# Six edits to a one-core, two-block transformer kernel: a second filling projection, every second convolution's projection in the eighth PSUM bank, and four moves of loads, stores and transposes

## The chip, the cores and the metric

The kernel runs on one core of one Trainium2 chip. The metric is the device time of one execution in microseconds; it was taken in three runs. The engines are called PE (TensorE: matmuls and transposes; its weight loads are PEld), ACT (ScalarE), DVE (VectorE), POOL (GpSimd) and SP (SyncE, which here only issues DMAs).

## What is computed

Sequence 512, width 1024, fp32. The first block has two layers; the second block has one.

```python
def first_block(x, ...):
    for layer in range(2):
        h = fox_attention(x, ...) if layer == 0 else diff_attention(x, k1, k2, v, ...)
        x = layer_norm(DN_ALPHA * x + h, ...)
        f = conv_ffn(x, ffn_w_in[layer], ffn_conv_w[layer], ffn_conv_b[layer], ffn_w_out[layer])
        x = layer_norm(DN_ALPHA * x + f, ...)
        if layer == 0: k1, k2, v = shared_kv(x, kv_w, cos, sin)

def second_block(x, ...):
    h = rms_norm(x, norm1_pre)
    q, k, v, z, xbc, dt_raw, gates = split_cols(h @ w_in, IN_SPLITS)
    q, k = axial_rope(rms_norm(q, q_norm), ...), axial_rope(rms_norm(k, k_norm), ...)
    attn_out = gqa_attention(q, k, v) @ w_attn_proj          # 8 query heads, 2 key heads
    ssd_y = ssd_branch(z, xbc, dt_raw, ...)                  # 5-tap convolution, silu, SSD both ways
    ssd_out = ssd_y @ w_ssd_proj
    g_attn, g_ssd = split(sigmoid(gates), 2)
    x = x + rms_norm((g_attn * attn_out + g_ssd * ssd_out) @ w_out, norm1_post)
    gate, up = split(rms_norm(x, norm2_pre) @ w_gate_up, 2)
    return x + rms_norm((silu(gate) * up) @ w_down, norm2_post)
```

## The kernel before

The sequence is held as four tiles of 128 rows (`t` = 0 to 3). Each fp32 product is made of three matmuls, since each operand is split into a high and a low part: weights come by SP's queue into `raw` (3 buffers, 512 KB each), ACT rounds them to `whi` (L185) and DVE makes the rest `wlo` (L186), 4 buffers of each. Activations are split in the same way (`split`, L193 on ACT and L194 on DVE). The transposed activations `xTh`, `xTl` come from `to_T` (L330) or `to_T2` (L1510): eight PE transposes of a tile, then L193 and L194.

PSUM has eight banks in three pools: `mm` with 3 banks (`psum()`), `at` with 4 (`psa()`), and `ms` with the eighth (`psm()`).

A scheduler writes the order of each engine's instructions from the program's text; each engine then runs its own list in order, and semaphores hold an instruction until what it reads is there and what it writes is free. Two things in the text steer that order. `later(t, f)` puts off the transposes of tile t, and `need(t)` issues those that are due; in `xs` the call is `need(t - self.depth)`, with `depth` 2. And `weave` takes turns between generators, so that filling work goes between the steps of an attention head.

The places that the change touches, in the order of time:

- `ffn` (L829), in both layers of the first block: `hook()` (L853) issues the loads of constants that the next stage uses (`load1`, `load2`), on POOL's queue, at group g = 1 of the up-projection.
- `run`, the end of layer 1's feed-forward (`post`, around L1591): after the layer norm of tile t, x is stored to DRAM (`xd`) by POOL's queue, and POOL computes the `pow` of the next norm (L1381, called by `rstd2`).
- `gqa` (L909 on): one projection gives k, v (`kv_epi`) and the first four q heads (`qgroup`), each through `norm_rope`. Then `F0` = 1 step of the filling work `fill` is issued, then k's transposes (L950, copied to `KT` by ACT at L952), then the eight heads: q's transposes (L957), scores (L543 and L544), `max` (DVE L965), `exp` (ACT L966), reciprocal (DVE L968), scaling (ACT L971, DVE L973), transposes of the probabilities (L401, split by L193 and L194) and the product with v (L985 and L986). Between those steps `fill` gives three steps a head: `ssd_convs`, 12 calls of `ssd_conv` (a projection of 24 matmuls, L217 to L219, into a PSUM bank; then ACT L1021, DVE L1025 four times, ACT L1027, DVE L1028), and between them transposes and products in the `ms` bank (L1112, L1117, L1125, copied by L1127 or split). After them come two gate projections. `ssd_scalars` uses `ms` too (L1077, L1078, L1090).
- `block2`, its end: `w_out` in two halves of 512 columns; in the second, tile by tile, `epi` does two norms (ACT L1341, DVE L1342, L1347, ACT L1349, POOL's `pow` L1381, ACT L1353), puts the transposes off by `later`, and stores x by POOL's queue (L1356, two per tile). `ffn2` follows at once: its first projections (`ws_pairs`, first) need tiles 0 and 1 of `xTh`, then tiles 2 and 3.
- `ffn2`, its end: the last rows of `w_down`, tile by tile; in `last` each tile's x is read back (L1545, POOL's queue) into one of two buffers `x2`, then the final norm and sum (L1549, twice a tile) and the stores of the result (L1550, SP's queue).

Of the kernel before, what the change touches and what calls it, by code (L numbers as in the profile page):

```python
# [8 lines left out]
F32 = mybir.dt.float32  # L9
# [7 lines left out]
D = 1024  # L17
P = 128
# [62 lines left out]
class K:  # L81
# [747 lines left out]
    def ffn(self, l, pool, make_post, hook):  # L829
        nc, I = self.nc, self.I  # L830
        W1, W2 = I["ffn_w_in"][l], I["ffn_w_out"][l]

        def conv(ps, m):
            y = pool.tile([P, S], F32, tag="cy", name="cy", bufs=4 - l)
            nc.scalar.activation(y, ps, AF.Identity, scale=self.c1(f"cw{l}2", m), bias=self.c1(f"cb{l}", m))  # L835
            for j, o in ((1, 1), (0, 2)):
                nc.vector.scalar_tensor_tensor(out=y[:, o:], in0=ps[:, :S - o], scalar=self.c1(f"cw{l}{j}", m), in1=y[:, o:], op0=ALU.mult, op1=ALU.add)  # L837
            return y

        def w_in(g):  # L840
            gc = self.ws_load(W1, g * 256)
            vc = self.ws_load(W1, DFF + g * 256)
            R = pool.tile([P, 2048], F32, tag="R", name="R", bufs=1)
            for i, gp, vp in self.ws_pairs(gc, vc, g == 0):
                y = conv(gp, 2 * g + i)
                nc.scalar.activation(y, y, AF.Silu)
                v = conv(vp, KF + 2 * g + i)
                nc.vector.tensor_tensor(out=R[:, i * 512:(i + 1) * 512], in0=y, in1=v, op=ALU.mult)
            if g == 0:
                for t in range(NT):  # L850
                    nc.scalar.activation(self.x[:, t, :], self.x[:, t, :], AF.Copy, scale=ALPHA)
            if g == 1:
                hook()  # L853
            return R

        def last():
            post = make_post()
            self.sums = [self.sm.tile([P, 3], F32, tag="sums", name="sums") for _ in range(NT)]
            self.ns = 2
            return lambda c: self.res_epi(c * 512, 512, 1.0, c, post if c else None)  # L860

        self.st_out(pool, W2, self.x, False, w_in, last)


# [148 lines left out]
    def ssd_conv(self, m):  # L1013

        nc = self.nc
        W = self.I["w_in_2"][0]
        ch = self.ws_load(W, 1792 + m * P, P)
        ps = self.psum()
        self.ws_mm(ps, ch, 0, self.xh, self.xl)
        y = self.unit()  # L1020
        nc.scalar.activation(y, ps, AF.Identity, scale=self.c1("c2w2", m), bias=self.c1("c2b", m))  # L1021
        for j in (0, 1, 3, 4):
            o = j - 2
            a, b = max(0, -o), S - max(0, o)
            nc.vector.scalar_tensor_tensor(out=y[:, a:b], in0=ps[:, a + o:b + o], scalar=self.c1(f"c2w{j}", m), in1=y[:, a:b], op0=ALU.mult, op1=ALU.add)  # L1025
        th = self.unit()
        nc.scalar.activation(th, y, AF.Tanh)  # L1027
        nc.vector.scalar_tensor_tensor(out=y, in0=th, scalar=1.0, in1=y, op0=ALU.add, op1=ALU.mult)  # L1028
        return y
# [202 lines left out]
    def block2(self, bpool):  # L1232
        nc, I, tc = self.nc, self.I, self.tc
# [33 lines left out]
        with tc.tile_pool(name="L", bufs=self.NL) as self.L:  # L1267
# [31 lines left out]
            with tc.tile_pool(name="mix", bufs=1) as pool:  # L1299
# [39 lines left out]
                def epi(c, t, ps):  # L1339
# [3 lines left out]
                    if c == 1:  # L1343
                        r = self.rstd2(sst[t])
                        ss = self.sm.tile([P, 2], F32, tag="ss4", name="ss4")
                        for i in range(2):
                            nc.vector.scalar_tensor_tensor(out=x[t][i], in0=mo[t][i], scalar=r, in1=x[t][i], op0=ALU.mult, op1=ALU.add)  # L1347
                            jk = pool.tile([P, S], F32, tag="jk", name="jk")
                            nc.scalar.activation(jk, x[t][i], AF.Square, scale=1.0 / 32, accum_out=ss[:, i:i + 1])  # L1349
                            nc.vector.tensor_tensor(out=mo[t][i], in0=x[t][i], in1=G2[:, i * 512:(i + 1) * 512], op=ALU.mult)  # L1350
                        r = self.rstd2(ss)
                        for i in range(2):
                            nc.scalar.activation(mo[t][i], mo[t][i], AF.Copy, scale=r)  # L1353
                        self.later(t, lambda: self.to_T2(mo[t], t))
                        for i in range(2):
                            nc.gpsimd.dma_start(xd[t, i], x[t][i])  # L1356
                for c in range(2):
                    self.xs(I["w_out_2"][0], c * 512, 512, KD, lambda k: mx[k][0], lambda k: mx[k][1], lambda t, ps, c=c: epi(c, t, ps), stagger=4 if c else 0)
        with tc.tile_pool(name="ffn2", bufs=1) as pool:
            self.ffn2(pool)  # L1360

    NL = 38
    F0 = 1
    depth = 2

    @staticmethod
# [147 lines left out]
    def ffn2(self, pool):  # L1514
        nc, I = self.nc, self.I
# [18 lines left out]
        def last(c):  # L1534
            sl = slice(c * 512, (c + 1) * 512)

            def epi(t, ps):
# [3 lines left out]
                nc.scalar.activation(jk, a, AF.Square, scale=1.0 / 32, accum_out=sst[t][:, c:c + 1])  # L1541
                nc.vector.tensor_tensor(out=a, in0=a, in1=G[:, sl], op=ALU.mult)
                if c == 1:
                    xt[t] = pool.tile([P, D], F32, tag="x2", name="x2", bufs=2)
                    nc.gpsimd.dma_start(xt[t], xd[t])  # L1545
                    r = self.rstd2(sst[t])
                    for i in range(2):
                        s = slice(i * 512, (i + 1) * 512)
# [1 line left out]
                        nc.sync.dma_start(self.out[t * P:(t + 1) * P, s], xt[t][:, s])  # L1550
            return epi

        self.st_out(pool, W2, acc, True, w_in, lambda: last)

    def run(self):
        nc, I, tc = self.nc, self.I, self.tc
# [3 lines left out]
        with tc.tile_pool(name="xp", bufs=1) as xp:  # L1560
# [19 lines left out]
            with tc.tile_pool(name="ffn1", bufs=1) as pool:  # L1580
# [4 lines left out]
                def make():  # L1585
# [2 lines left out]

                    def post(t):
                        self.layer_norm(t, G, B, jk)  # L1590
                        nc.gpsimd.dma_start(xd[t], self.x[:, t, :])  # L1591
                        h = pool.tile([P, D], F32, tag="Q", name="Q", bufs=4)
                        ss = self.sm.tile([P, 2], F32, tag="ss4", name="ss4")
                        for i in range(2):
# [39 lines left out]
```

## Time and profile before

| | |
|---|---|
| median of 3 runs | 2091.38 us (2090.37 to 2091.85) |
| the profiled execution | 2091.34 us |
| its span in the trace | 2089.6 us |
| granted TensorE clock, mean over the span | 0.995 |
| PE busy | 2038.2 us (98%) |
| DVE, ACT, POOL busy | 74%, 52%, 4% |

The trace shows the span; the profiled execution is 1.7 us longer than that. A row of a timeline gives an instruction's start, its duration and, in brackets, how long its engine had been idle before it and whose end released it. A matmul's duration is that of a pipelined instruction: the next one starts before it ends, so the step from start to start is what one costs. In `<-` the output stands on the left.

### The profile page before, as it was taken

How to read it: one execution, taken by the hardware profiler on the slowest of the kernel's cores; microseconds unless marked ns; L12 is line 12 of the kernel's file. 1: busy time of each engine (PE TensorE's matmuls, PEld its weight loads, DVE VectorE, ACT ScalarE, POOL GpSimd, SP SyncE). 2: the span in 40 equal slices, each digit the busy share in tenths (PEclk: the TensorE clock that was granted, in tenths of full speed). 3: DMA queues.
4: the chain of work that ended last, by engine and by line, in shares of the span. 5: the costliest groups of instructions: out<-in, count | busy, mean ns of one | idle time of the engine just before them, and what ended most of it. 6: DMA issues, size and time to landing. Idle time of an engine off the chain costs nothing.

```text
span 2089.6 us, 28051 instructions
## 1 busy us (share of the span) xinstructions
PE 2038.2 (98%) x10563; PEld 1724.7 (83%) x10563; DVE 1554.7 (74%) x2776; ACT 1085.3 (52%) x1905; POOL 75.6 (4%) x113
## 2 busy tenths in 40 slices
PE   8999999999999999999999998999999999999998
PEld 7888888888888789888888887887898878888886
DVE  5777878788956888777887866997798544575564
ACT  4777655444435977455444344676475343443322
POOL 0000000000000000010000011000000010000000
PEclk9999999999999999999999999999999999999999
DMA  6221242233223221252224332211323425222322
GB/s 170 62 61 61 71 139 85 77 121 121 84 88 91 71 71 51 66 166 83 76 86 131 101 117 78 72 31 36 106 61 98 144 91 185 97 90 72 121 81 91
DMA packets 197470, 193.71 MB, mean 93 GB/s; under 512 B 8934, under 2 KB 170455, under 8 KB 197335
## 3 DMA queue, kind: packets, MB, share of 16 engines
q1 hardware_dynamic: 191398, 173.04, 26.9%
q0 software_dynamic: 5504, 17.31, 2.7%
q8 instruction: 83, 1.36, 0.3%
q10 hardware_dynamic: 432, 1.57, 0.2%
q14 instruction: 53, 0.43, 0.1%
HBM read 185.61 MB, written 6.29 MB: 92 GB/s over the span
## 4 chain that ended last, share of the span: by engine, by line
PE 80%; DVE 8%; ACT 7%; issue 3%; POOL 1%; DMA 1%; POOLq 0%; DVEq 0%; ACTq 0%; SPq 0%
PE mm L219 15%; PE mm L218 15%; PE mm L217 15%; PE mm L293 3%; PE mm L291 3%; PE mm L292 3%; PE at L1437 3%; PE at L1438 3%; PE at L1439 3%; PE at L401 2%; DVE wlo L186 1%; ACT sw L699 1%; PE mm L1437 1%; PE mm L1438 1%; PE mm L1439 1%
## 5 line engine op out<-in xcount | busy, mean ns | idle before, releaser
L217 PE MATMUL mm<-xTh,whi 128*128 128x512 f32 (+1 forms) x1584 | 605.4, 383 | 8.2 <-ACT xTh L193 5.6
L219 PE MATMUL mm<-xTh,wlo 128*128 128x512 f32 (+1 forms) x1584 | 604.2, 382 | 1.2 <-DVE wlo L186 1.2
L218 PE MATMUL mm<-xTl,whi 128*128 128x512 f32 (+1 forms) x1584 | 604.6, 382 | 0.1
L185 ACT ACTIVATE whi<-raw 128x1024 fp32r<-128x1024 f32 (+3 forms) x282 | 293.2, 1044 | 316.2 <-PE mm L218 174.6
L186 DVE TENSOR_TENSOR wlo<-raw,whi 128x1024 fp32r<-128x1024 f32 (+3 forms) x282 | 337.1, 1199 | 146.0 <-ACT whi L185 140.2
L217 PEld LDWEIGHTS mm<-xTh,whi 128*128 128x128 f32 x1584 | 298.9, 189 | 63.3 <-ACT xTh L193 6.1
L219 PEld LDWEIGHTS mm<-xTh,wlo 128*128 128x128 f32 x1584 | 298.8, 189 | 57.6 <-DVE wlo L186 2.1
L218 PEld LDWEIGHTS mm<-xTl,whi 128*128 128x128 f32 x1584 | 299.1, 189 | 54.7 <-DVE xTl L194 0.3
L837 DVE SCALAR_TENSOR_TENSOR cy<-mm,cols,cy 128x511 f32<-128x511 f32 (+1 forms) x172 | 128.3, 746 | 67.3 <-ACT cy L835 65.3
L193 ACT ACTIVATE whi<-wr 128x1024 fp32r<-128x1024 f32 x84 | 89.0, 1060 | 90.2 <-PE mm L218 29.1
L293 PE MATMUL mm<-whi,xTl 128*128 128x256 f32 x416 | 119.0, 286 | 1.7 <-DVE xTl L194 1.0
L291 PE MATMUL mm<-whi,xTh 128*128 128x256 f32 x416 | 119.2, 287 | 1.1 <-ACT xTh L193 1.1
L835 ACT ACTIVATE cy<-mm,cols 128x512 f32<-128x512 f32 x86 | 66.5, 773 | 103.1 <-PE mm L219 103.1
L292 PE MATMUL mm<-wlo,xTh 128*128 128x256 f32 x416 | 118.3, 285 | 0.0
L194 DVE TENSOR_TENSOR wlo<-wr,whi 128x1024 fp32r<-128x1024 f32 x84 | 101.9, 1220 | 12.9 <-ACT whi L193 12.0
L193 ACT ACTIVATE hh<-R 128x256 fp32r<-128x256 f32 (+2 forms) x57 | 54.9, 963 | 85.4 <-DVE R L1528 43.2
L1438 PE MATMUL at<-wlo,hh 128*128 128x512 f32 x240 | 93.4, 389 | 0.0
L1439 PE MATMUL at<-whi,hl 128*128 128x512 f32 x240 | 93.4, 389 | 0.0
L1437 PE MATMUL at<-whi,hh 128*128 128x512 f32 x240 | 92.7, 389 | 0.0
L193 ACT ACTIVATE ph<-at 128x512 fp32r<-128x512 f32 (+3 forms) x128 | 58.6, 474 | 54.2 <-PE at L401 40.7
L293 PEld LDWEIGHTS mm<-whi,xTl 128*128 128x128 f32 x416 | 80.2, 193 | 3.4 <-DVE xTl L194 1.9
L291 PEld LDWEIGHTS mm<-whi,xTh 128*128 128x128 f32 x416 | 80.2, 193 | 2.6 <-ACT xTh L193 1.8
(451 smaller groups left out, 3850.5 us busy)
## 6 DMA issues: line engine op xcount, KB each, us to landing
raw<-in_ffn_w_in_dram SPq DMA_DIRECT2D x88, 512.0 KB
raw<-in_w_gate_up_dram SPq DMA_DIRECT2D x44, 512.0 KB
raw<-in_w_in_dram SPq DMA_DIRECT2D x40, 512.0 KB
wr<-in_ffn_w_out_dram SPq DMA_DIRECT2D x32, 512.0 KB
raw<-in_a_w_in_dram SPq DMA_DIRECT2D x22, 512.0 KB
raw<-in_kv_w_dram SPq DMA_DIRECT2D x16, 512.0 KB
wr<-in_w_down_dram SPq DMA_DIRECT2D x16, 512.0 KB
raw<-in_ffn_w_out_dram SPq DMA_DIRECT2D x12, 512.0 KB
```

The source lines that it names most:

```text
L185: nc.scalar.activation(hi, raw, AF.Copy)
L186: nc.vector.tensor_tensor(out=lo, in0=raw, in1=hi.bitcast(F32), op=ALU.subtract)
L193: nc.scalar.activation(hi, src, AF.Copy)
L217: mm(o, wh, a, start=(k == 0), stop=False)
L218: mm(o, wh, b, start=False, stop=False)
L219: mm(o, wl, a, start=False, stop=(k == ktiles - 1))
L291: mm(o, a, hi[:, kk, :], start=(k == 0 and t % 2 == 0), stop=False)
L292: mm(o, a, lo[:, kk, :], start=False, stop=False)
L293: mm(o, b, hi[:, kk, :], start=False, stop=(k == ktiles - 1 and t % 2 == 1))
L1437: mm(ps[t], a, wh, start=p == 0, stop=False)
L1438: mm(ps[t], a, wl, start=False, stop=False)
L1439: mm(ps[t], b, wh, start=False, stop=p == 1)
```

## The change

- `hook()` is called at g = 4 instead of g = 1.
- `ssd_conv` takes its bank from `ms` for odd m, from `mm` for even m (the order of the calls is m = 8, 10, 0, 1, 2, 3, 9, 11, 4, 5, 6, 7).
- `F0` is 2: two filling projections are issued ahead of k's transposes.
- x is stored from SP's queue instead of POOL's, in layer 1's `post` and in `block2`'s `epi`.
- `depth` is 1 from `w_out` on.
- The four reads of x at the end of `ffn2` are issued together ahead of the last projection (`ends`), into two tiles of the ring `R`; the buffers `x2` are gone.

```diff
--- before.py
+++ after.py
@@ -849,7 +849,7 @@
             if g == 0:
                 for t in range(NT):
                     nc.scalar.activation(self.x[:, t, :], self.x[:, t, :], AF.Copy, scale=ALPHA)
-            if g == 1:
+            if g == 4:
                 hook()
             return R
 
@@ -1015,7 +1015,7 @@
         nc = self.nc
         W = self.I["w_in_2"][0]
         ch = self.ws_load(W, 1792 + m * P, P)
-        ps = self.psum()
+        ps = self.psm() if m % 2 else self.psum()
         self.ws_mm(ps, ch, 0, self.xh, self.xl)
         y = self.unit()
         nc.scalar.activation(y, ps, AF.Identity, scale=self.c1("c2w2", m), bias=self.c1("c2b", m))
@@ -1353,14 +1353,15 @@
                             nc.scalar.activation(mo[t][i], mo[t][i], AF.Copy, scale=r)
                         self.later(t, lambda: self.to_T2(mo[t], t))
                         for i in range(2):
-                            nc.gpsimd.dma_start(xd[t, i], x[t][i])
+                            nc.sync.dma_start(xd[t, i], x[t][i])
+                self.depth = 1
                 for c in range(2):
                     self.xs(I["w_out_2"][0], c * 512, 512, KD, lambda k: mx[k][0], lambda k: mx[k][1], lambda t, ps, c=c: epi(c, t, ps), stagger=4 if c else 0)
         with tc.tile_pool(name="ffn2", bufs=1) as pool:
             self.ffn2(pool)
 
     NL = 38
-    F0 = 1
+    F0 = 2
     depth = 2
 
     @staticmethod
@@ -1541,8 +1542,6 @@
                 nc.scalar.activation(jk, a, AF.Square, scale=1.0 / 32, accum_out=sst[t][:, c:c + 1])
                 nc.vector.tensor_tensor(out=a, in0=a, in1=G[:, sl], op=ALU.mult)
                 if c == 1:
-                    xt[t] = pool.tile([P, D], F32, tag="x2", name="x2", bufs=2)
-                    nc.gpsimd.dma_start(xt[t], xd[t])
                     r = self.rstd2(sst[t])
                     for i in range(2):
                         s = slice(i * 512, (i + 1) * 512)
@@ -1550,7 +1549,15 @@
                         nc.sync.dma_start(self.out[t * P:(t + 1) * P, s], xt[t][:, s])
             return epi
 
-        self.st_out(pool, W2, acc, True, w_in, lambda: last)
+        def ends():
+            for i in range(2):
+                R = pool.tile([P, 2048], F32, tag="R", name="R", bufs=2)
+                for t in (2 * i, 2 * i + 1):
+                    xt[t] = R[:, t % 2 * D:(t % 2 + 1) * D]
+                    nc.gpsimd.dma_start(xt[t], xd[t])
+            return last
+
+        self.st_out(pool, W2, acc, True, w_in, ends)
 
     def run(self):
         nc, I, tc = self.nc, self.I, self.tc
@@ -1588,7 +1595,7 @@
 
                     def post(t):
                         self.layer_norm(t, G, B, jk)
-                        nc.gpsimd.dma_start(xd[t], self.x[:, t, :])
+                        nc.sync.dma_start(xd[t], self.x[:, t, :])
                         h = pool.tile([P, D], F32, tag="Q", name="Q", bufs=4)
                         ss = self.sm.tile([P, 2], F32, tag="ss4", name="ss4")
                         for i in range(2):
```

PE in the middle of the eight heads, around the first products of `ssd_scalars` (L1077); L217 to L219 on `mm` are filling projections. Before:

```order
L217 MATMUL mm<-xTh,whi 128x512
L986 MATMUL at<-pl,L 128x512
L543 MATMUL at<-L,A 128x512
L544 MATMUL at<-L,A 128x512
L985 MATMUL at<-ph,L 128x512
L218 MATMUL mm<-xTl,whi 128x512
L1077 MATMUL ms<-L,c_sums 128x64 x2
L1078 MATMUL ms<-L,c_sums 128x128
L219 MATMUL mm<-xTh,wlo 128x512
L543 MATMUL at<-L,A 128x512
L544 MATMUL at<-L,A 128x512
L217 MATMUL mm<-xTh,whi 128x512
```

After (line numbers before L1356 are the same):

```order
L543 MATMUL at<-L,A 128x512
L986 MATMUL at<-pl,L 128x512
L544 MATMUL at<-L,A 128x512
L957 MATMUL at<-ident,L 128x128 x4
L401 MATMUL at<-ident,Pt 128x128 x8
L1077 MATMUL ms<-L,c_sums 128x64 x2
L1078 MATMUL ms<-L,c_sums 128x128
L985 MATMUL at<-ph,L 128x512
L986 MATMUL at<-pl,L 128x512
L543 MATMUL at<-L,A 128x512
L544 MATMUL at<-L,A 128x512
L985 MATMUL at<-ph,L 128x512
```

Before, matmuls of a filling projection stand between the steps of the head; after, at this place, none do from the L401 rows ahead of this piece on until the projection into `ms` that follows it. Over the whole program PE has as many instructions as before, and so have DVE and ACT.

ACT from the second half of `w_out` into `ffn2` (L1341, L1349, L1353: the epilogue of a tile; L193 `xTh`: the split of a transposed tile; L185: weights). Before:

```order
L1353 ACTIVATE L<-L,ss_16064 128x512 x2
L1341 ACTIVATE jk,ss_15859<-mm 128x512
L1349 ACTIVATE jk,ss_16103<-L 128x512 x2
L1353 ACTIVATE L<-L,ss_16113 128x512 x2
L1341 ACTIVATE jk,ss_15860<-mm 128x512
L193 ACTIVATE xTh<-at 128x4x128 x2
L185 ACTIVATE whi<-raw 128x1024
L1349 ACTIVATE jk,ss_16152<-L 128x512
L185 ACTIVATE whi<-raw 128x1024
L1349 ACTIVATE jk,ss_16152<-L 128x512
L185 ACTIVATE whi<-raw 128x1024
L1353 ACTIVATE L<-L,ss_16162 128x512 x2
```

After:

```order
L1353 ACTIVATE L<-L,ss_16064 128x512 x2
L1341 ACTIVATE jk,ss_15859<-mm 128x512
L193 ACTIVATE xTh<-at 128x4x128 x2
L1349 ACTIVATE jk,ss_16103<-L 128x512 x2
L1353 ACTIVATE L<-L,ss_16113 128x512 x2
L1341 ACTIVATE jk,ss_15860<-mm 128x512
L193 ACTIVATE xTh<-at 128x4x128 x2
L185 ACTIVATE whi<-raw 128x1024
L1349 ACTIVATE jk,ss_16166<-L 128x512
L185 ACTIVATE whi<-raw 128x1024
L1349 ACTIVATE jk,ss_16166<-L 128x512
L185 ACTIVATE whi<-raw 128x1024
```

Before, the first split of a transposed tile comes after the third tile's L1341 and the second (three rows further on) after the third tile's L1353; after, the splits of tiles 0 and 1 come behind the L1341 of tiles 1 and 2. On PE the eight transposes of tile 0 stand behind 48 matmuls of the second half instead of 72.

POOL at the end of `ffn2` (`ss` rows: one `pow` per tile). Before:

```order
L1381 TENSOR_TENSOR ss_16225<-ss_16224,mhalf 128x1
L353 DMA G<-in_norm_post_dram 128x1024
L1545 DMA x_18667<-xd 128x1024
L1545 DMA x_18700<-xd 128x1024
L1381 TENSOR_TENSOR ss_18670<-ss_18669,mhalf 128x1
L1381 TENSOR_TENSOR ss_18703<-ss_18702,mhalf 128x1
L1545 DMA x_18733<-xd 128x1024
L1381 TENSOR_TENSOR ss_18736<-ss_18735,mhalf 128x1
L1545 DMA x_18766<-xd 128x1024
L1381 TENSOR_TENSOR ss_18769<-ss_18768,mhalf 128x1
```

After, where L1381 is L1382 and L1545 is L1557:

```order
L1382 TENSOR_TENSOR ss_16239<-ss_16238,mhalf 128x1
L353 DMA G<-in_norm_post_dram 128x1024
L1557 DMA R<-xd 128x1024 x4
L1382 TENSOR_TENSOR ss_18674<-ss_18673,mhalf 128x1
L1382 TENSOR_TENSOR ss_18705<-ss_18704,mhalf 128x1
L1382 TENSOR_TENSOR ss_18736<-ss_18735,mhalf 128x1
L1382 TENSOR_TENSOR ss_18767<-ss_18766,mhalf 128x1
```

The four reads stand ahead of all the `pow`s. On SP's queue the eight stores L1356 stand among the loads of `ffn2`: three loads, six stores, three loads, two stores, two loads.

## Rows read from the trace of the kernel before

**Rows 1.** Page, part 1: busy time of each engine and share of the span.

```profile
PE 2038.2 (98%) x10563; PEld 1724.7 (83%) x10563; DVE 1554.7 (74%) x2776; ACT 1085.3 (52%) x1905; POOL 75.6 (4%) x113
```

**Rows 2.** PE timeline, w_out to ffn2: start us, us, instruction, idle before it.

```profile
1707.12 0.39 PE L257 MATMUL mm<-whi,L 128*128 128x512 f32 x1
...
1712.57 1.03 PE L1510 MATMUL at<-ident,L 128*128 128x128 f32 x8
...
1725.25 0.98 PE L217 MATMUL mm<-xTh,whi 128*128 128x256 f32 x3 [5.31 <-ACT xTh L193]
...
1740.62 0.62 PE L217 MATMUL mm<-xTh,whi 128*128 128x256 f32 x3 [0.30 <-ACT xTh L193]
```

**Rows 3.** Windows, all engines: length, busy us, then PEclk, DMA share, GB/s.

```profile
1236.00:1266.00 30.00, 26.54 (x191) 23.90 (x191) 24.68 (x47) 17.07 (x37) 7.13 (x11) 1.00 0.37 121
1271.00:1274.60 3.60, 3.60 (x19) 3.60 (x19) 1.69 (x4) 0.05 (x1) 1.65 (x1) 0.55 0.72 192
1299.00:1302.50 3.50, 3.50 (x14) 3.11 (x13) 0.00 (x0) 3.48 (x7) 0.00 (x0) 0.56 0.00 0
1360.00:1400.00 40.00, 40.00 (x214) 32.55 (x213) 38.17 (x74) 28.99 (x71) 0.00 (x0) 1.00 0.05 15
1725.00:1729.00 4.00, 3.75 (x18) 3.75 (x19) 3.87 (x8) 3.38 (x7) 1.67 (x3) 0.57 1.02 332
```

**Rows 4.** ACT timeline, the same stretch.

```profile
1707.60 1.34 ACT L1353 ACTIVATE L<-L,ss 128x512 f32<-128x512 f32 x2 [1.11 <-POOL ss L1381]
...
1714.45 1.34 ACT L1353 ACTIVATE L<-L,ss 128x512 f32<-128x512 f32 x2 [1.11 <-POOL ss L1381]
...
1722.80 1.33 ACT L1353 ACTIVATE L<-L,ss 128x512 f32<-128x512 f32 x2 [0.85 <-POOL ss L1381]
...
1724.61 1.07 ACT L193 ACTIVATE xTh<-at 128x512 fp32r<-128x512 f32 x2
```

**Rows 5.** POOL timeline, the stores at 1257 and 1705, and the last issue of the tail.

```profile
1257.86 0.58 POOL L1591 DMA_DIRECT2D xd<-x  x1 [1.74 <-DVE x L381]
1258.83 0.56 POOL L1381 TENSOR_TENSOR ss<-ss,mhalf 128x1 f32<-128x1 f32 x1 [0.39 <-DVE ss L1380]
...
1705.21 1.21 POOL L1356 DMA_DIRECT2D xd<-L  x2 [1.08 <-DVE L L1347]
1707.00 0.56 POOL L1381 TENSOR_TENSOR ss<-ss,mhalf 128x1 f32<-128x1 f32 x1 [0.58 <-DVE ss L1380]
...
2080.57 0.57 POOL L1545 DMA_DIRECT2D x<-xd  x1 [1.84 <-DMA out_dram<-x]
```

**Rows 6.** SP queue timeline, start of ffn2.

```profile
1722.41 8.67 SPq L183 DMA_DIRECT2D raw<-in_w_gate_up_dram  x4
```

**Rows 7.** DVE timeline, the tail.

```profile
2070.02 1.42 DVE L1549 SCALAR_TENSOR_TENSOR x<-acc,ss,x 128x512 f32<-128x512 f32 x2 [0.74 <-POOL ss L1381]
...
2082.24 0.15 DVE L1380 SCALAR_TENSOR_TENSOR ss<-ss 128x1 f32<-128x1 f32 x1
2084.76 1.42 DVE L1549 SCALAR_TENSOR_TENSOR x<-acc,ss,x 128x512 f32<-128x512 f32 x2 [2.37 <-issue]
```

**Rows 8.** PE timeline around k's transposes, 1269 to 1299.

```profile
1269.09 1.99 PE L950 MATMUL at<-ident,L 128*128 128x128 f32 x8 [2.35 <-ACT L L923]
...
1297.58 0.47 PE L217 MATMUL mm<-xTh,whi 128*128 128x512 f32 x1 [1.21 <-DVE L L1025]
1298.70 0.69 PE L957 MATMUL at<-ident,L 128*128 128x128 f32 x2 [0.64 <-ACT L L952]
```

**Rows 9.** DVE timeline, reciprocals of two successive heads.

```profile
1425.67 0.18 DVE L968 RECIPROCAL s<-s 128x4 f32<-128x4 f32 x1 [0.65 <-ACT Pt L966]
...
1436.79 0.18 DVE L968 RECIPROCAL s<-s 128x4 f32<-128x4 f32 x1 [0.59 <-ACT Pt L966]
```

**Rows 10.** ACT and DVE by line, 1304 to 1450: xcount, busy us, mean ns, idle before.

```profile
L1021 ACT ACTIVATE L<-mm,cols 128x512 f32<-128x512 f32 x10 | 7.8, 779 | 0.0
...
L1127 ACT ACTIVATE L<-ms 128x128 f32<-128x128 f32 x32 | 6.4, 293 | 1.3 <-PE ms L1125 1.2
...
L1025 DVE SCALAR_TENSOR_TENSOR L<-mm,cols,L 128x510 f32<-128x510 f32 (+1 forms) x44 | 32.6, 740 | 1.0 <-ACT L L1021 0.9
```

**Rows 11.** Waits of PE, 1225 to 1450: us, times, longest.

```profile
PE at L401 <- DVE Pt L973: 0.8, 1, 0.8
```

## Prediction

> **What bounds the kernel.** I read the page's first part, then PE's waits, then the timelines of the three places where the change moves PE's work or the end of the program. PE is busy 98% of the span [rows 1], so the reader should look for the little that PE does not do: a stall of PE, what arrives last at it, and what the clock does afterwards. No instruction is added on PE, DVE or ACT; only order, queues and banks move. The three places are **A**, the grouped attention of the second block (1225 to 1450 us), **B**, the passage from `w_out` into `ffn2` (1707 to 1741), and **C**, the tail.
>
> Two things hold for all of them. First, a 128x512 matmul costs 0.227 us: 24 of them run from 1707.12 to 1712.57 [rows 2]. Eight 128x128 transposes take 1.03 us as a row [rows 2], of which the last one's overlap is hidden; about 0.108 us each. Second, a long stall costs twice. After the idle 2.35 us before L950 [rows 8] the granted clock is 0.55 over the next 3.6 us, and after the 5.31 us of B [rows 2] it is 0.57 over 4 us, which is its lower level (1.2 of 2.4 GHz) for most of that time [rows 3]; about 3.4 us at half speed loses 1.7 us. The stretch 1236 to 1266 holds 3.5 us of idle PE in smaller pieces and keeps the clock at 1.00 [rows 3].
>
> **The change part by part, against the profiled execution of 2091.34 us** (the median of the runs shown is 2091.38, so the two agree to 0.04).
>
> *Hook.* The order of every engine is the same there with g = 4 as with g = 1: the loads wait for their memory, not for their place in the text. Cost and gain 0.
>
> *Stores from SP instead of POOL.* A pair of stores holds POOL for 1.21 us, a single one for 0.58 [rows 5]. The `pow` behind them would profit if it waited for them, but in both places POOL is idle 0.58 and 0.39 us before it and DVE's sum releases it [rows 5]. So the stores are already covered: 0. On SP they stand in front of weight loads; at `ffn2` the six stores follow three loads, and the fourth load starts at 1722.41 [rows 6], while tile 2's x is ready at about 1718.9: tile 0's pair starts at 1705.21 [rows 5], and a tile takes 6.85 us (L1353 at 1707.60 and 1714.45 [rows 4]). Six issues have 3.5 us to go out. Cost 0 as well. The bounds: nothing gained, nothing lost; if this cover were gone, one tile's chain would move by at most the 1.21 us pair.
>
> *B, depth 1.* Before, tile 1's transposes are ready by 1720, but their split L193 stands on ACT behind L1353 of tile 2, which runs 1722.80 to 1724.13; so L193 starts at 1724.61 [rows 4] and PE stands 5.31 us, then 0.30 us more at 1740.62 [rows 2]. With the lost clock B costs 5.31 + 0.30 + 1.7 = 7.3 us. After, the transposes of a tile come one tile earlier, and the splits stand ahead of the next tile's norms. PE is free after 48 matmuls at 1707.12, and tile 0's normed halves are there at 1708.27 and 1708.94 (L1353, two instructions from 1707.60 [rows 4]): with the first four transposes run in between, a wait of 1.45 us. The next 24 matmuls end at 1714.9; tile 1's L1353 ends at 1715.79: 0.5 us. The last 24 end at 1721.75, and the first products of `ffn2` follow, with some 0.3 us for a low part of the weights. Tile 2's transposes then meet a norm that ends at about 1724.8 (0.7 us later than now, since L1341 of tile 3 goes first): 1.4 us. Together 3.65 us, in pieces that are each shorter than the stalls after which rows 3 show a low clock. **B: -3.6 us**; -1.9 if a low stretch comes again, -4.5 if tile 2 is as early as now.
>
> *C, early reads.* The last read is issued at 2080.57 after a wait of 1.84 us for a store to free its buffer [rows 5], and the last L1549 starts at 2084.76, with 2.37 us idle before it [rows 7]. In the other tiles L1549 starts 0.9 us after L1380 (its 0.15 us and 0.74 of waiting for `pow` [rows 7]); L1380 of the last tile is at 2082.24, so with x there it starts at 2083.14. **C: -1.6 us.** The reads now go out ahead of the last projection, whose 144 matmuls of 0.227 us last 32.7 us, eight times the 4.2 us from the last issue to L1549. The bounds: 0 if the ring `R` were not free until then, 2.37 if `pow` were not needed.
>
> *A, filling projection and eighth bank.* Three terms.
>
> (1) The filling projections come earlier, and those in the shared bank wait for its other users, so that one head runs out of filling. From the last score of the head before it to its own last score, of which the piece of PE's order shows the end, PE has 26 matmuls of 128x512 (ten of them filling, all in front) and 20 transposes: 26 x 0.227 + 20 x 0.108 = 8.06 us. How fast a head can go when PE has little else is seen near the end of the heads: from reciprocal to reciprocal 1425.67 to 1436.79, 11.1 us [rows 9]. Cost 11.1 - 8.06, **+3.1 us**. At the very place, 0.43 us of transposes (L957 x4) stand between the last score and the L401 that wait for its softmax. Bounds: 0, if PE arrives so late that the softmax is ready; 4.8, if the stall also lowers the clock.
>
> (2) The `ms` bank is a single one, now with six projections in a row with its transposes. After such a projection it is held for L1021 and four L1025, 0.78 + 4 x 0.74 = 3.74 us [rows 10], before the next user may write; after L1125 for four copies L1127 of 0.29 [rows 10]. The order puts 3.8 to 6.8 us of PE work between a projection and the next user of the bank, so the bank is just about free in time; DVE's own queue, busy 38.17 of 40 us in the middle of the heads [rows 3], makes it late by some tenths. I take +0.3 us for each of the six, **+1.8**, with 0 and 6 (1 us each) as ends.
>
> (3) What may be gained. The wait for k's norms, 2.35 us, stays: L950 comes at the same place as before, and its releaser L923 depends on the projection, not on filling [rows 8]. The wait of 1.21 us for L1025 at 1297.58 [rows 8] is for one of the three `mm` banks; after, the fourth filling projection in `mm` waits for the same bank, so it stays, and the 0.64 us behind it too. One wait of 0.8 us for the scaled probabilities [rows 11] gets more work in front of it. **-0.8.**
>
> The Trainium skill, Perfetto Trace Analysis, Matmul Optimizations, says that all eight PSUM banks should be used, to have most work ready at a time; that would turn (1) and (2) into gains. No run here shows a projection in the eighth bank, and by that rule the time is that of the first rival.
>
> A: 3.1 + 1.8 - 0.8 = **+4.1 us**. Sum: 2091.34 - 3.6 - 1.6 + 4.1 = **2090.2 us**. Its own range, with A from +1 to +6 and B from -4.5 to -1.9: 2086.2 to 2093.8.
>
> **The rivals.** *The eighth bank pays* (faster). The stretch without filling costs nothing, since the stalls that I expect in the heads are hidden by PE's arriving later, and the bank is never late: 2091.34 - 3.6 - 1.6 - 0.8 = 2085.3. If the stall at 1297.58 goes as well, with its 1.21, 0.64 and the 1.7 of the low clock behind it (0.56 from 1299 [rows 3]), it is 2081.8. For it: that wait is truly for a bank. Against it: the piece of the order without filling.
>
> *The eighth bank starves PE* (slower). Each of the six projections in `ms` makes its next user wait 1 us, and the bare stretch ends in a low clock: 6 + 3.1 + 1.7 = 10.8, so 2091.34 - 5.2 + 10.8 = 2096.9. It decides from A = +9.4. For it: DVE is busy 95% of the time from 1360 to 1400 [rows 3], so 3.74 us are the least. Against it: the bank's occupation (six times 5.4 + 3.7, and the small users) is well below the 146 us of the heads.
>
> *B's waits merge.* If tiles 0 to 2 stall PE so that the clock falls again, B gives 1.9: 2091.34 - 1.9 - 1.6 + 4.1 = 2091.9, no change.
>
> *The change does nothing in B*: the order shows the moves, so only if tile 2's norm is late by 5 us; it is within the last rival.
>
> **How the numbers follow.** About 0.2% (4.2 us) is what a measurement of this kernel can tell from no change: faster is below 2087.2, slower above 2095.6. Chances: my forecast 0.48, the bank pays 0.26, the bank starves PE 0.15, B merges 0.11. Faster: nearly all of the first rival and the lowest eighth of the forecast, 0.31; slower: most of the second rival and a remainder, 0.15; the same 0.54. The range reaches into both rivals, from 2084.0 to 2096.0 and leaves out the outer parts of both, about 0.17.
>
> **What would show it.** The 5.31 us wait of L217 gone, with waits of 0.3 to 1.5 us at L1510 (then L1511) in its place and PEclk 1.00 behind them; the last L1549 (L1548 after the change) 0.9 us behind DVE's L1380 (then L1381); the waits for L950 and L1025 still there; and a new wait of about 3 us at L401 where the order has no filling. I am wrong if PE's waits inside the heads add up to nothing (first rival), or if PE waits for L1025 or L1127 at L1112, L1125 or at a projection into `ms` by more than 3 us in all (second).

## The result, and the profile after

The changed kernel takes 2122.7 us (median of 4 runs, 2121.58 to 2123.91) against 2091.43 for the kernel before on the same chip (4 runs): a ratio of 1.0151, interval 1.0139 to 1.0164. It is slower by 31.3 us, far above the range of the prediction. The profiled execution took 2121.63 us, its span 2119.6, with a mean granted clock of 0.992.

The page's part 1, after:

```profile
PE 2050.5 (97%) x10563; PEld 1731.1 (82%) x10563; DVE 1556.0 (73%) x2776; ACT 1086.1 (51%) x1905; POOL 68.6 (3%) x101
```

Against [rows 1] every engine has the work that it had, but for the twelve stores that SP's queue has taken over from POOL, and PE runs the same number of instructions. So the two traces can be laid side by side: the start of PE's n-th instruction after, less that of its n-th before, tells how late the changed kernel is there. (The order within a stretch differs, so this is read at the ends of the stretches.)

| PE's place, us of the trace after | late by, us | what PE has passed by then |
|---|---|---|
| 1200 | +0.3 | the hook; layer 1's `post` is next |
| 1277 | +0.4 | F0 = 2, k's transposes |
| 1322 | +2.2 | first head |
| 1372 | +14.9 | heads 2 to 4 |
| 1422 | +26.6 | heads 5 and 6 |
| 1475 to 1730 | +35.3 | end of the heads; then nothing until `w_out` |
| 1769 | +31.7 | **B** |
| 2074 | +31.6 | `ffn2` |
| end of span | +30.0 | **C** |

So A is +35, B is -3.6 and C -1.6. All of the loss lies in the heads. The next lines are windows of the trace after, cut where PE is at the same instruction as at 1320, 1357, 1395 and 1439.70 before (columns: length, busy us with instructions of PE, PEld, DVE, ACT, POOL, then PEclk, DMA share, GB/s):

```profile
1322.20:1371.90 49.70, 41.80 (x204) 31.14 (x202) 40.31 (x84) 28.65 (x64) 4.13 (x4) 0.93 0.20 53
1371.90:1421.60 49.70, 42.49 (x200) 33.31 (x199) 29.56 (x56) 23.51 (x51) 0.00 (x0) 0.97 0.11 28
1421.60:1475.00 53.40, 46.78 (x225) 35.15 (x222) 39.20 (x67) 32.64 (x76) 0.00 (x0) 0.97 0.13 34
```

and the same three of the kernel before:

```profile
1320.00:1357.00 37.00, 35.83 (x204) 29.65 (x204) 33.08 (x70) 23.39 (x51) 4.15 (x4) 1.00 0.27 72
1357.00:1395.00 38.00, 38.00 (x201) 30.77 (x200) 36.19 (x70) 26.22 (x61) 0.00 (x0) 1.00 0.10 29
1395.00:1439.70 44.70, 44.55 (x226) 33.81 (x225) 36.88 (x65) 32.58 (x79) 0.00 (x0) 1.00 0.18 48
```

The three stretches grow from 119.7 to 152.8 us, by 33.1. PE's idle time grows from 1.3 to 21.7, and its busy time by 12.7: about 6.6 us of that is the lower clock (0.07 of 49.7, 0.03 of 49.7 and of 53.4), the rest I have not divided. DVE too is busy for a smaller share than before (109.1 of 152.8 us against 106.2 of 119.7). No engine became the bound; the engines wait for each other.

What they wait for, after, from 1300 to 1485 (us in total, times, longest). PE:

```profile
PE at L401 <- ACT Pt L971: 7.8, 4, 4.0
PE at L986 <- DVE pl L194: 3.2, 3, 1.3
PE at L401 <- ACT Pt L966: 2.3, 2, 1.2
...
PE at L957 <- ACT Pt L966: 1.4, 2, 1.0
```

ACT, and DVE:

```profile
ACT whi L185 <- PE ms L218: 22.7, 6, 4.6
ACT L L1027 <- DVE L L1025: 13.8, 6, 3.4
```

```profile
DVE wlo L186 <- ACT whi L185: 14.5, 4, 4.9
DVE pl L194 <- ACT ph L193: 12.0, 11, 3.4
DVE m L965 <- PE at L544: 7.3, 2, 4.8
```

In the kernel before PE waits in the heads for 0.8 us at L401 [rows 11] and little else. After, it waits for the softmax of its head (L966, L971), and ACT, in six places, for the end of a projection into `ms`. One such round, PE from 1424 to 1441:

```profile
1424.64 0.60 PE L957 MATMUL at<-ident,L 128*128 128x128 f32 x4
1429.27 1.28 PE L401 MATMUL at<-ident,Pt 128*128 128x128 f32 x6 [4.03 <-ACT Pt L971]
...
1434.63 0.50 PE L217 MATMUL ms<-xTh,whi 128*128 128x512 f32 x1
...
1440.00 0.39 PE L219 MATMUL ms<-xTh,wlo 128*128 128x512 f32 x1
1440.22 0.39 PE L985 MATMUL at<-ph,L 128*128 128x512 f32 x1
```

ACT and DVE in the same time:

```profile
1434.47 1.08 ACT L193 ACTIVATE ph<-at 128x512 fp32r<-128x512 f32 x2
1440.20 0.63 ACT L185 ACTIVATE whi<-raw 128x512 fp32r<-128x512 f32 x1 [4.64 <-PE ms L218]
```

```profile
1435.10 1.29 DVE L194 TENSOR_TENSOR pl<-at,ph 128x512 fp32r<-128x512 f32 x2 [2.89 <-ACT ph L193]
1440.86 0.69 DVE L186 TENSOR_TENSOR wlo<-raw,whi 128x512 fp32r<-128x512 f32 x1 [4.48 <-ACT whi L185]
```

The engines take turns. From 1425.24 the next in PE's list are transposes of probabilities that ACT and DVE have not made yet: 4.03 us idle, with filling in the list behind them. Then come the transposes, and a little later in PE's list all 24 matmuls of a projection into `ms`, without a gap, from 1434.63 to 1440.22. The next step of the head, L985, has its operands split on DVE by 1436.39, but stands behind those 24. And while they run, ACT and DVE are idle for 4.6 and 4.5 us, ACT for a weight buffer that the projection still reads.

How the filling lies in the heads, counted in the two traces from the last score matmul (L544) of a head to that of the next: length in us, matmuls of L217 to L219 in it, and PE's idle time. (Another projection, L257 to L259 with 96 matmuls of 128x288, lies here too: 22 and 74 of them in heads 2 and 3 before, 38 and 48 after.)

| head | 2 | 3 | 4 | 5 | 6 | 7 | 8 | sum |
|---|---|---|---|---|---|---|---|---|
| before, us | 20.2 | 23.2 | 25.4 | 19.3 | 15.5 | 15.8 | 11.4 | 130.8 |
| filling | 43 | 28 | 74 | 42 | 38 | 36 | 19 | 280 |
| PE idle, us | 0 | 0 | 1.1 | 0 | 0 | 0 | 0 | 1.1 |
| after, us | 24.4 | 21.2 | 15.9 | 29.5 | 23.7 | 25.8 | 19.3 | 159.8 |
| filling | 24 | 14 | 10 | 72 | 48 | 48 | 42 | 258 |
| PE idle, us | 3.6 | 3.1 | 3.2 | 3.5 | 4.0 | 4.2 | 1.8 | 23.4 |
| granted clock | 0.93 | 1.00 | 0.79 | 0.94 | 1.00 | 0.93 | 1.00 | |

Heads 2 to 4 lose 97 matmuls, at 0.227 us 22.0 us of work, but become only 7.3 us shorter. Heads 5 to 8 get 75 more, 17.0 us, and become 36.3 us longer. In these seven heads the filling lies in 55 pieces before, of which 2 have 20 matmuls or more (at most 23); after, in 31 pieces, of which 6 have 24 or more. Before, the granted clock is 1.00 in each head.

B after, PE's four passages:

```profile
1743.67 1.27 PE L1511 MATMUL at<-ident,L 128*128 128x128 f32 x8 [1.06 <-ACT L L1353]
...
1750.51 1.27 PE L1511 MATMUL at<-ident,L 128*128 128x128 f32 x8
...
1759.93 0.66 PE L1511 MATMUL at<-ident,L 128*128 128x128 f32 x4 [0.93 <-ACT L L1353]
...
1760.55 0.66 PE L1511 MATMUL at<-ident,L 128*128 128x128 f32 x4
```

C after, DVE's last tile:

```profile
2113.76 0.15 DVE L1381 SCALAR_TENSOR_TENSOR ss<-ss 128x1 f32<-128x1 f32 x1
2114.64 1.41 DVE L1548 SCALAR_TENSOR_TENSOR R<-acc,ss,R 128x512 f32<-128x512 f32 x2 [0.73 <-POOL ss L1382]
```

The stall of 5.31 us [rows 2] has become waits of 1.06 and 0.93, and the last tile's sum starts 0.88 us after L1381, where 2.37 us were idle before [rows 7].

### The profile page after: what moved, and what is told of

Read it like the earlier page. It is cut to its first block, busy times and chain, and to the rows that moved or that the text cites. A ratio compares the mean times of both kernels' runs of the same rounds, so it can differ in the third digit from the quotient of the medians.

```text
span 2119.6 us, 28057 instructions
## 1 busy us (share of the span) xinstructions
PE 2050.5 (97%) x10563; PEld 1731.1 (82%) x10563; DVE 1556.0 (73%) x2776; ACT 1086.1 (51%) x1905; POOL 68.6 (3%) x101
## 4 chain that ended last, share of the span: by engine, by line
PE 80%; DVE 9%; ACT 7%; issue 2%; POOL 1%; DMA 1%; POOLq 0%; DVEq 0%; ACTq 0%; SPq 0%
PE mm L217 15%; PE mm L219 15%; PE mm L218 15%; PE mm L293 3%; PE mm L291 3%; PE mm L292 3%; PE at L1438 3%; PE at L1439 3%; PE at L1440 3%; PE at L401 1%; DVE wlo L186 1%; PE mm L257 1%; PE mm L258 1%; PE mm L259 1%; ACT sw L699 1%
## 5 line engine op out<-in xcount | busy, mean ns | idle before, releaser
L217 PE MATMUL mm<-xTh,whi 128*128 128x512 f32 (+1 forms) x1536 | 586.2, 382 | 2.8 <-DVE Pt L465 1.3
L219 PE MATMUL mm<-xTh,wlo 128*128 128x512 f32 (+1 forms) x1536 | 585.2, 382 | 2.1 <-DVE wlo L186 2.0
L218 PE MATMUL mm<-xTl,whi 128*128 128x512 f32 (+1 forms) x1536 | 585.5, 381 | 0.0
L185 ACT ACTIVATE whi<-raw 128x1024 fp32r<-128x1024 f32 (+3 forms) x282 | 293.2, 1044 | 336.8 <-PE mm L218 170.9
L219 PEld LDWEIGHTS mm<-xTh,wlo 128*128 128x128 f32 x1536 | 289.7, 189 | 58.0 <-DVE wlo L186 4.0
L217 PEld LDWEIGHTS mm<-xTh,whi 128*128 128x128 f32 x1536 | 289.4, 189 | 55.9 <-issue 1.5
L218 PEld LDWEIGHTS mm<-xTl,whi 128*128 128x128 f32 x1536 | 289.7, 189 | 53.1 <-DVE xTl L194 0.2
L193 ACT ACTIVATE whi<-wr 128x1024 fp32r<-128x1024 f32 x84 | 89.0, 1060 | 90.2 <-PE mm L218 29.1
L193 ACT ACTIVATE hh<-R 128x256 fp32r<-128x256 f32 (+2 forms) x57 | 54.9, 964 | 83.1 <-DVE R L1529 41.9
L193 ACT ACTIVATE ph<-at 128x512 fp32r<-128x512 f32 (+3 forms) x128 | 58.3, 475 | 48.9 <-PE at L401 34.9
```

The costliest lines, as they stand in the source:

```text
L185: nc.scalar.activation(hi, raw, AF.Copy)
L193: nc.scalar.activation(hi, src, AF.Copy)
L217: mm(o, wh, a, start=(k == 0), stop=False)
L218: mm(o, wh, b, start=False, stop=False)
L219: mm(o, wl, a, start=False, stop=(k == ktiles - 1))
```

## The experiments

In all of them "the four moves" is the changed kernel without the second filling projection ahead of the heads and without the eighth bank. Each kernel is compared with the kernel before on the same chip; the chip is not the same for all tables and pairs, so differences between them carry the spread of the kernel before (2090.91 to 2091.52 us). Three questions: which part costs it, what about the bank costs it, and what would get it back.

### Which part: the four moves, F0, the eighth bank

The four moves alone:

```diff
-        ps = self.psm() if m % 2 else self.psum()
+        ps = self.psum()
-    F0 = 2
+    F0 = 1
```

> The four moves alone (hook, stores, depth, early reads), F0 = 1 and all convolutions in mm. All theories: B gives 3.6 us and C 1.6 us as in the trace of the change, so about 2086.2 us against 2091.4 before; if the moves also slow the heads, 2095 or more.

The four moves and F0 = 2:

```diff
-        ps = self.psm() if m % 2 else self.psum()
+        ps = self.psum()
```

> The four moves and F0 = 2, all convolutions in mm. Theory 'block' (the loss comes from the projections in the shared eighth bank): 2086 to 2090 us, at most some 3 us over the four moves. Rival 'early' (the filling is spent ahead of k's transposes, so the heads run bare): 2105 us or more.

The four moves and the eighth bank:

```diff
-    F0 = 2
+    F0 = 1
```

> The four moves and every second convolution in ms, F0 = 1. Theory 'block': nearly the whole loss, 2115 to 2123 us. Rival 'early': 2087 to 2096 us.

| | us | ratio to before (2091.07) | over the four moves |
|---|---|---|---|
| four moves | 2086.62 | 0.9977 [0.9969, 0.9986] | |
| and F0 = 2 | 2089.75 | 0.9996 [0.9987, 1.0005] | +3.1 |
| and the eighth bank | 2119.41 | 1.0134 [1.0120, 1.0148] | +32.8 |

The loss is the bank's: all three times lie where the theory 'block' had them. F0 and the bank together, 35.9, are what the whole change costs over the four moves (31.3 + 4.45 = 35.8), so the parts hardly interact. PE's waits with the bank alone have the pattern of the whole change:

```profile
PE at L401 <- ACT Pt L971: 6.2, 3, 3.1
PE at L985 <- ACT ph L193: 5.0, 8, 1.3
PE at L986 <- DVE pl L194: 2.8, 3, 1.5
PE ms L1125 <- DVE L L1025: 2.0, 1, 2.0
PE ms L1125 <- DVE L L1028: 1.7, 1, 1.7
```

### What about the bank: its other users, the wait for L1077, the number of projections

The whole change, with the small users of `ms` in `ssd_convs` (L1112, L1117, L1125) in `at`, so that the projections share the bank with `ssd_scalars` alone:

```diff
-            pt = self.psm()
+            pt = self.psa()
```

(in three places)

> The whole change, but B's transposes and products and x's transposes (L1112, L1117, L1125) take a bank of at instead of ms, so that the eighth bank serves the odd convolutions nearly alone. Theory 'block' in the form that the sharing of one bank in a series is the cause: 2088 to 2098 us. If any projection in the eighth bank is to blame, shared or not: 2115 us or more.

2119.97 us, ratio 1.0139 [1.0125, 1.0153], as the second expectation had it: next to nothing came back. It isn't a clean test: the moved users load the `at` banks, which the heads need, and a wait that was not there takes the old ones' place:

```profile
PE ms L1077 <- DVE L L1074: 4.1, 1, 4.1
```

The bank is idle for 40 us in the trace after, from 1336.64 (L1127) to L1077 at 1376.50; from there on it is taken almost without a gap until the last L1127 ends at 1466.38. Its five projections start 13.6 to 23.5 us apart, and each of the last four starts within 0.06 us of the end of the instruction that read the bank before it (1393.95 and 1394.00, 1411.07 and 1411.11, 1434.58 and 1434.63, 1451.02 and 1451.08). So the bank is one row of 90 us, behind a wait of 40 us. The next theory was that this chain waits for `ssd_scalars`. The whole change, with the scalars issued two heads later:

```diff
-                late = scalars
+            if h == 3:
+                late = scalars
```

> The whole change, but the scalars of the SSD (L1077, L1090, which take the ms bank) begin after head 3 instead of head 1. Theory 'chain': the one ms bank is handed on in the program's order, so convolution 3 and all filling behind it wait some 40 us (1336.64 to 1376.50) for L1077, whose inputs are late; with L1077 later in the program this wait goes and the time falls to 2088 to 2098 us. Rival 'block' (projections in one bank are always issued as late blocks of 24, whatever stands ahead of them): 2113 us or more.

and the same edit on the four moves, as its control:

> Control: the four moves alone (F0 = 1, all convolutions in mm), with the scalars begun after head 3. Both theories: within 2 us of the four moves, 2084.6 to 2088.6 us, since nothing but small transposes waits behind L1077 there.

2119.65 us, 1.0135 [1.0122, 1.0149], against 2090.46, 0.9993 [0.9984, 1.0002] for the control (2 us above what was expected of it): 29.2 us remain of a difference of 36, where 'chain' had most of it gone. The third head has 34 filling matmuls instead of 14 and the fourth 32 instead of 10, but the eighth then takes 30.6 us. The wait for L1077 decides where the filling is missing; four fifths of the time are lost without it.

One projection alone in the eighth bank, that of m = 1 or of m = 3 (on the four moves):

```diff
-        ps = self.psm() if m % 2 else self.psum()
+        ps = self.psm() if m == 1 else self.psum()
```

> The four moves, and of all convolutions m = 1 alone in ms: in the program's order it stands ahead of L1077. Theory 'chain': 2086 to 2089 us. Rival 'block', a sixth of the 32.8 us: 2091 to 2093 us.

> The four moves, and of all convolutions m = 3 alone in ms: in the program's order it stands behind L1077. Theory 'chain': the filling behind it waits for L1077 too, 2095 to 2115 us, far more than m = 1 costs. Rival 'block': 2091 to 2093 us, as m = 1.

2096.14 us (1.0024 [1.0014, 1.0033]), which is 9.5 over the four moves and above what any theory gave, and 2100.5 us (1.0040 [1.0027, 1.0052]), 13.9 over: in the range of 'chain', but not far more than m = 1 costs. With m = 1 alone no projection stands behind L1077; PE is still idle for 5.0 us in the heads, among them:

```profile
PE at L401 <- ACT Pt L971: 2.0, 2, 1.8
```

In its trace the 24 matmuls stand in one piece again, from 1319.69 to 1325.17. With m = 3 one head gets 72 filling matmuls and takes 34.8 us. Two of the six projections cost 23.4 us, if the two add up; all six cost 32.8, so they don't cost equally.

### Is it what stands behind the projection: weight splits on ACT

ACT's longest wait after, 22.7 us in six times, is L185 for a weight buffer that a projection into `ms` still reads; softmax stands behind it in ACT's list. So the splits of the filling's weights were put on POOL, which is idle there, in the whole change and in the four moves:

```diff
-        nc.scalar.activation(hi, raw, AF.Copy)
-        nc.vector.tensor_tensor(out=lo, in0=raw, in1=hi.bitcast(F32), op=ALU.subtract)
+        nc.gpsimd.tensor_copy(hi, raw)
+        nc.gpsimd.tensor_tensor(out=lo, in0=raw, in1=hi.bitcast(F32), op=ALU.subtract)
```

(in short; for `ssd_conv` and the first two gate projections)

> The whole change, but POOL instead of ACT and DVE splits the weights of the filling projections (L185, L186), so that ACT and DVE no longer stand behind a projection in ms with a split that waits for its weight buffer. The blocks of 24 in PE's order stay. Theory 'queue' (ACT's L185 waits 22.7 us in the heads for projections in ms, and the softmax chains stand behind it on ACT, then DVE): at most 16 us over its control e10, some 2090 to 2102 us. Rival 'block' (PE's order leaves the heads bare, whatever ACT waits for): 25 us or more over e10.

> Control: the four moves alone with the same splits on POOL. Both theories: near the four moves, 2083 to 2093 us, unless POOL is too slow for the weights (each split on POOL over 5 us), which would show in both kernels as waits of PE for POOL.

2137.51 us (1.0223 [1.0208, 1.0238]) and 2111.45 (1.0091 [1.0074, 1.0108]): both are slower than expected, and 26.1 us of difference remain of some 36, as 'block' had it. The wait left L185, and came back at the next instruction of ACT that needs the projection:

```profile
ACT L L1021 <- PE ms L219: 19.7, 4, 5.8
```

So the weight splits are not the main cause, though they may carry a part of it; POOL slowed both kernels too much to tell how large a part.

### How long the bank is held: a copy

If the loss comes from the bank's being held by L1021 and four L1025, a copy into SBUF frees it sooner. On the eighth bank alone, on that with the scalars later, and on the four moves as the control:

```diff
+        if m % 2:
+            cp = self.unit()
+            nc.scalar.activation(cp, ps, AF.Copy)
+            ps = cp
```

> The four moves and every second convolution in ms (as the run of 2119.4 us), but ACT copies the projection out of ms at once and the taps read the copy, so that the bank is held for some 1.5 us after a projection instead of 6. Theory 'late' (one bank with a slow hand-over makes each projection come late, so that it stands as the oldest work in PE's order, runs as one block of 24, and no longer lies between a head's steps): half of the loss goes, 2096 to 2108 us. Rival 'block' (whatever stands in a single bank comes in blocks): 2113 us or more.

> As the copy kernel, and the scalars begin after head 3, so that neither the taps nor L1077 hold the bank. Theory 'late': most of the loss goes, 2088 to 2102 us. Rival 'block': 2113 us or more.

> Control: the four moves with the same six copies, all projections in mm. All theories: 2086 to 2092 us (six copies of 0.6 us on ACT, which is not the bound).

| | us | ratio to before (2091.39) | over the control |
|---|---|---|---|
| control: four moves and copies | 2091.21 | 0.9998 [0.9989, 1.0007] | |
| eighth bank and copies | 2111.79 | 1.0098 [1.0084, 1.0112] | +20.6 |
| and the scalars two heads later | 2106.09 | 1.0070 [1.0058, 1.0083] | +14.9 |

The bank's cost falls from 32.8 to 20.6 when it is held for less long, and to 14.9 when the scalars don't stand in its row either (11.1, if the 3.8 that this move costs the four moves are taken off). So the time for which the one bank is held is part of the cost, 12 us of 33; both times lie between the ranges of the two theories, and neither accounts for the rest. In the control ACT waits 12.4 us for projections in `mm` at L185, eight times, and PE stays busy:

```profile
ACT whi L185 <- PE mm L218: 12.4, 8, 4.1
```

So a wait of ACT behind a projection does no harm by itself; that it does where PE has nothing else to go on with is argued, not shown.

Counted as above, PE's idle time in the seven heads and the loss over the four moves or the control:

| kernel | PE idle, us | loss, us |
|---|---|---|
| copies in `mm` (control) | 2.4 | 0 |
| m = 1 alone | 5.0 | 9.5 |
| m = 3 alone | 10.8 | 13.9 |
| copies, scalars later | 16.0 | 14.9 |
| copies | 17.8 | 20.6 |
| all odd m | 23.0 | 32.8 |

The loss grows with PE's idle time in the heads, in this order in all six. Two more kernels with the bank don't fit the count of seven heads: the whole change with later scalars (17.1 idle, 29.2 over its control) and with the small users in `at` (18.1, 33.4 over the four moves). Counted over the whole stretch instead, for the same instructions of PE as from 1275 to 1480 before, their idle time is 21.9 and 25.6 us, against 4.2 before, 19.9 with copies and 28.4 with all odd m; there the order holds but for the last two, whose losses are 0.6 us apart. Their granted clock in that stretch is 0.94, that of the kernel before 0.99.

## Why the prediction was wrong

**What held.** Hook and stores: at 1277 us PE is late by 0.4, predicted 0. B: -3.6, predicted -3.6, though in two waits of 1.06 and 0.93 rather than 1.45, 0.5 and 1.4; the clock is 1.00 behind them (1743 to 1747, 1760 to 1764), as forecast. C: -1.6, predicted -1.6. By the runs, the four moves together give 4.45 us (2086.62 against 2091.07); predicted were 5.2. The waits for L950 (2.5 us) and L1025 (up to 1.9) stayed, as A(3) said.

**What failed: A, predicted +4.1, measured +35.** The step is A(1). There I set PE's work in a head, 8.06 us, against the head's own length, 11.1 [rows 9], and took the greater: as long as PE has more work than 11.1 us in a head, the head would hide behind it. I looked for heads with less work than that and counted one, with a stall of 3.1 us. In the trace after PE stands idle in all seven heads, 1.8 to 4.2 us each, 23.4 in all, and in four of them the granted clock is lower, for which the forecast had nothing.

The account that fits is that the greater of the two is right only where the work lies *between* the steps of the head. After the change it lies in pieces of 24, and a piece that comes when the head's next step is ready delays that step by its whole length, and stands there for all of the softmax that PE later waits for. Heads 6 and 7 show it: 48 filling matmuls each, and by the numbers of A 18.0 and 18.4 us of PE work, more than 11.1, so I had 0 for them. PE was idle in them for 4.0 and 4.2 us, and they took 23.7 and 25.8. The sum, 11.1 + 48 x 0.227 = 22.0, is nearer to that than the maximum; for head 5 with 72 it gives 27.4, measured 29.5. In the kernel before, the same sum for head 5, with 42, is 20.6 and for head 6, with 38, is 19.7; they took 19.3 and 15.5, with PE never idle: there the filling lies within the head's length. The piece of order that I read was the right one, and so was "a new wait of about 3 us at L401": there are four to L971, the longest 4.0, not one. But I read the order for a head without filling, and not for heads with all of it in one piece.

The 11.1 us itself was misread. PE does not have "little else" there; it is busy for the whole of it, and 20 of its matmuls in it are filling:

```profile
1425.67:1436.79 11.12, 11.12 (x53) 7.75 (x52) 7.80 (x14) 7.25 (x16) 0.00 (x0) 1.00 0.13 40
```

So 11.1 is PE's work in that stretch, and no run shows what a head takes alone; the sums above are rough, and hold some filling twice. Head 4 after, whose order I had read, was idle for 3.2 us where 11.1 - 8.06 gave 3.1. That agreement is luck, and the head took 15.9 us and not 11.1, at a granted clock of 0.79.

A(2) was sized wrongly too, in its kind: I priced the `ms` bank by what its next user would wait, 0.3 us each. Those waits stayed small, about 1.3 us in all from 1300 to 1485 (3.7 with the bank alone), so the sign that I had named for the slower rival, over 3 us of them, did not come in the changed kernel:

```profile
PE ms L217 <- ACT L L1127: 0.5, 1, 0.5
PE ms L1125 <- DVE L L1025: 0.5, 1, 0.5
PE ms L1112 <- DVE L L1025: 0.3, 1, 0.3
```

The bank's price is paid elsewhere. While a projection has to wait for its turn in the bank, the filling behind it in the text isn't there for the heads either, and the order of PE has nothing to put in its place: heads 2 to 4 have 48 filling matmuls instead of 145. The slower rival named the right bank and the right side, but by the mechanism of A(2) with 1 us instead of 0.3, so it ended at 2096.9, a fifth of the loss. Its argument against itself, that the bank is busy for well below the heads' 146 us, counted the bank's time as a sum, 9.1 us a projection, and not as a row in which one projection waits for the next: from 1380.40 to 1451.08 they start 17.7 us apart on average.

The Trainium skill, Perfetto Trace Analysis, Matmul Optimizations, has it that all eight PSUM banks be used. Here the one projection in two that went into the eighth bank cost 32.8 us. The bank was in use before as well, for short products, so the rule holds for both kernels; read as in the prediction, as a gain from projections in that bank, it and the measurement differ, and the measurement decides.

**Shown**: that the eighth bank causes the loss, and neither F0 (3.1) nor the four moves (-4.45); that it falls by 12 us when the bank is held for less long; that it is lost as PE's idle time and a lower clock in the heads (20.4 and about 6.6 of 33.1 us in the three stretches), with the filling in long pieces. **Argued only**: that the pieces in PE's order make the loss, rather than come with it; the order was not tried with the bank and the pieces broken up. **Open**: what makes the 11 to 15 us that are left with the copy and the later scalars, and why m = 1 alone costs 9.5. A second bank for these projections was not tried, so that one bank is too few for them is argued as well.

The best version of those measured is the four moves alone, with `F0` = 1 and all convolutions in `mm`: 2086.62 us, 0.9977 of the kernel before.

## What to carry to other kernels

In these heads filling work hid a latency where it lay between the steps of the chain, and not where it lay in long pieces; so count, in the engine's order, how long the pieces of filling are and which step of the chain stands behind each, not how much work a stage has. A bank of its own for results that are held for long (a projection of 5.6 us and then 3.7 us of reading) put them in one row; here the time was lost not where its users wait, but where the filling behind them was missing. Of several edits in one change, measure the parts apart: here four of them gained 4.5 us, and two lost 36.

## What was not expected of the hardware

POOL is not a free engine for elementwise work here. In the four moves with POOL's weight splits, by line, 1290 to 1500 (count, busy us, mean ns):

```profile
L186 POOL TENSOR_TENSOR wlo<-raw,whi 128x1024 fp32r<-128x1024 f32 x10 | 24.7, 2471 | 0.6
...
L185 POOL CAST whi<-raw 128x1024 fp32r<-128x1024 f32 x10 | 10.7, 1078 | 64.7 <-PE mm L218 62.9 <-issue 1.8
```

The copy takes 1.08 us, the subtraction 2.47. And DVE becomes slower in the same stretch of the program: an unchanged sum of q's rotation, 1250 to 1450, with POOL's splits and then in the kernel before:

```profile
L906 DVE TENSOR_TENSOR L<-L,stq 128x256 f32<-128x256 f32 x8 | 8.6, 1070 | 0.0
```

```profile
L906 DVE TENSOR_TENSOR L<-L,stq 128x256 f32<-128x256 f32 x8 | 3.3, 417 | 0.0
```

The mean of 1070 ns mixes two cases. The five of the eight beside which POOL splits nothing take 0.42 us, as before; one beside a copy takes 1.25, and two beside a subtraction 2.61 each. Such a one, DVE and POOL:

```profile
1296.38 2.61 DVE L906 TENSOR_TENSOR L<-L,stq 128x256 f32<-128x256 f32 x1
```

```profile
1296.26 2.45 POOL L186 TENSOR_TENSOR wlo<-raw,whi 128x1024 fp32r<-128x1024 f32 x1
```

It ends 0.28 us after POOL's subtraction. L1025, which reads PSUM, is not slower in this kernel: 0.75 us at most in 48, as in the kernel before. The wait of PE for k's norms grows as well, from 2.35 us [rows 8] to 6.9:

```profile
PE at L950 <- ACT L L923: 10.5, 2, 6.9
```

The control of that pair is itself slower by 20 us, in part by such waits, and so the pair tells less than it was meant to.
